# Stick-breaking attention in a two-layer streaming encoder: one query block at a time against two

## The chip, the cores and the metric

The kernel runs on one core of a Trainium2 chip. The metric is the device time of one launch in microseconds. The core has five engines with queues of their own: TensorE (PE, with its weight loads PEld), VectorE (DVE), ScalarE (ACT), GpSimd (POOL) and SyncE (SP, which here only issues transfers). TensorE writes to PSUM, which has eight banks of 512 fp32 columns each.

## The reference

Two layers run over 512 prompt tokens and 32 sample tokens together (544 columns in the kernel). In each layer one input projection feeds four token mixers (stick-breaking attention, retention, forgetting attention "fox", and sparse attention "dsa" on the 128 keys that an indexer selects), whose outputs are gated and summed; then come an output projection, a layer norm, a feed-forward and a second layer norm. The part that matters is the stick-breaking mixer, 4 heads of 64, with queries and keys in blocks of 128:

```
z = einsum('bqhd,blhd->bhql', q, k) * 64 ** -0.5
earlier = kpos[None, :] < qpos[:, None]
log_1mb = where(earlier, log_sigmoid(-z), 0.0)
after = cumsum(log_1mb, axis=3, reverse=True) - log_1mb      # sum over the later keys
w = where(earlier, exp(log_sigmoid(z) + after), 0.0)
y = einsum('bhql,blhd->bqhd', w, v)
```

Since `log_sigmoid(z) = z + log_sigmoid(-z)`, the exponent is `z` plus a sum of `log_sigmoid(-z)` over this key and all later ones, up to the query.

## The kernel before

**Precision.** Most products use the form fp32r, with each operand split in a high and a low part: a product is then two or three matmuls of the split parts. Each of these matmuls comes with its own load of 128x128 weights (the columns PE and PEld of the page have the same number of instructions).

**The stick-breaking mixer** (`stick`, line 1434). Keys stand on the partitions, queries on the free axis. For a query block `i` (128 queries), heads are taken in two passes `s` (0, 1), each with two heads `p`. The key blocks `j = i .. 0` are taken two at a time in "units"; a unit has one PSUM bank `z`, with 256 columns (2 heads x 128 queries) for each key block. In a unit:

- TensorE writes the mask (`sbmask`, bf16, only for the diagonal block) and, per key block and head, the logits: two matmuls of 128 columns (`sq` against the high part `sk` and the low part `skl` of the keys).
- `stick_unit` (line 1421) makes `log(1+exp(z))`: ACT Abs, Exp and Ln, a DVE operation (`sa`), an ACT copy to the high part of `hl` and a POOL subtraction for the low part of `hl`.
- `select` lets DVE do two steps of the indexer's top-k that waits to be done.
- TensorE adds the suffix sums to the same bank: the triangle `trin` against the block's own `hl`, and the all-minus-one matrix `onen` against the `hl` of every later key block, each for the high and the low part, 256 columns a time.
- ACT takes Exp to `sw`; the bank is then free for the next unit.

After both passes, `sw` and the values `svt` are multiplied in bank 7 (`so`), and `ev_heads` copies the result to `y_sb`. A unit's PSUM bank is one of two (`z=(4, 5)` in `BANKS`, line 106), which the indexer, fox, dsa and retention use too.

**The order of the work.** The program is recorded, not issued at once: every call becomes an entry with the entries it depends on, and `Plan.schedule` (line 553) sorts all of them for all engines by priority (the place in the program, less an offset), its own costs and the moment when operands are ready. So the stick mixer's matmuls stand between those of the projections that follow (fox, dsa). Places in SBUF are chosen from a draft of the same plan, so a change in one mixer can move entries anywhere. `Plan.fillers` (line 635) puts small bf16 matmuls (`idle`, line 657) where the plan has TensorE waiting. Nearly all instructions are issued from line 659, so the trace is read by tile names.

Names that come up below: `whi`, `wlo` (split weights of a projection, 272 columns a matmul, one half of the 544 tokens), `wop` (weights of the Strassen products in gates and feed-forward), `wb` (branch weights in `merge`), `T`, `T_plain` (differences of the halves of h for the Strassen products, made on POOL in `h_differences`, line 1699), `ikh`, `ikl`, `iq` (indexer), `fu`, `pT` (fox softmax), `oc`, `kd`, `S`, `rk` (retention, line 1541), `C,lf` (cumulative forget sums). The first layer is layer 0, the second layer 1.

Of the kernel before, what the change touches and what calls it, by code (L numbers as in the profile page):

```python
# [14 lines left out]
AF = mybir.ActivationFunctionType  # L15
# [649 lines left out]
class Build:  # L665
# [768 lines left out]
    def stick(self, q, qb, k, svt):  # L1434
        nc = self.nc
# [3 lines left out]
        for i in range(4):  # L1439
            blocks = list(range(i, -1, -1))  # L1440
            units = [tuple(blocks[a:a + 2]) for a in range(0, len(blocks), 2)]
            W = {}
            for s in range(2):
                r = slice(s * 64, s * 64 + 64)
                later = []
                for un in units:
                    n = 256 * len(un)
                    z = self.tps("sz")
                    first = True
                    if i in un:  # L1450
                        nc.tensor.matmul(z[:, :256], self.B["ident"],
# [3 lines left out]
                    for x, j in enumerate(un):  # L1455
                        for p in range(2):
                            c = (2 * x + p) * 128
                            self.z(z[:, c:c + 128], q, ks, 2 * p + s, slice(i * 128, (i + 1) * 128),
                                   slice(j * 128, (j + 1) * 128), first, True)
                            first = False  # L1460
                    hl = self.stick_unit(z, n)
                    self.select(SELECT[1])
                    own = [(hl, 256 * x) for x in range(len(un))]
                    for x, j in enumerate(un):
                        for src, a, lhs in [(*own[x], self.trin)] + [(*b, self.onen) for b in later + own[:x]]:
                            for part in range(2):
                                nc.tensor.matmul(z[:, 256 * x:256 * x + 256], lhs, src[:, part, a:a + 256], start=False,
                                                 stop=True, skip_group_check=True)
                    later = later + own
                    w = self.w512("sw")  # L1470
                    nc.scalar.activation(w[:, :n], z[:, :n], AF.Exp)
                    for x, j in enumerate(un):
                        W[s, j] = (w, 256 * x)
            o = self.aps("so")
            for p in range(2):
                for s in range(2):
                    h = 2 * p + s
                    for j in range(i + 1):
                        w, a = W[s, j]
# [608 lines left out]
```

## Time and profile before

| | |
|---|---|
| median of 3 runs | 1942.51 us (1942.05 to 1944.62) |
| the profiled execution | 1938.36 us, its span 1936.6 us |
| TensorE busy | 1871.6 us of the span (97%), 14658 matmuls |
| VectorE, ScalarE, GpSimd busy | 1607.1 (83%), 1053.3 (54%), 498.8 us (26%) |
| mean granted TensorE clock | 0.995 of 2.4 GHz |

Times in the trace are microseconds from the span's start. A matmul's row gives its whole passage; matmuls overlap, so what one costs TensorE is the distance from its start to the next one's start. A number in brackets with an arrow is how long the engine sat idle before a row, and who released it. The layers' stick mixers lie at 88 to 160 us and at 1050 to 1126 us.

### The profile page before, as it was taken

To read this page: it belongs to the slowest core of one execution; us is meant where nothing else is said; L and a number is where in the kernel's file an instruction comes from. 1 tells how busy PE (TensorE), PEld (TensorE's weight loads), DVE (VectorE), ACT (ScalarE), POOL (GpSimd) and SP (SyncE) were. 2 spreads that over 40 slices of the span, in tenths; PEclk is the share of its full clock that TensorE was granted. 3 is DMA by queue.
4 is the path that set the end of the run, shared out by engine and by line. 5 is a ranking of instruction groups with operands and counts; after the bars stand their busy time and mean duration, and the time that the engine had idled before them with its cause. 6 is when DMAs were issued, how large, how long until landed. Compare 5 with 4: busy or idle time off the path is not lost.

```text
span 1936.6 us, 39257 instructions
## 1 busy us (share of the span) xinstructions
PE 1871.6 (97%) x14658; PEld 1815.8 (94%) x14658; DVE 1607.1 (83%) x3566; ACT 1053.3 (54%) x2183; POOL 498.8 (26%) x500
## 2 busy tenths in 40 slices
PE   9999999999999999999999999999999999999997
PEld 8998898999999999999989989999999999999996
DVE  5988768887879989988789796687788799899875
ACT  4465533555637656556465563365556475565552
POOL 0343031143441111321413421312434301114101
PEclk9999999999999999999999999999999999999999
DMA  8222243667542587776413222346665237777741
GB/s 229 79 64 81 55 101 75 153 142 163 145 124 77 135 195 174 170 180 169 130 23 95 60 84 68 78 107 159 151 154 155 86 86 169 188 174 175 171 114 47
DMA packets 387423, 241.38 MB, mean 125 GB/s; under 512 B 27272, under 2 KB 363576, under 8 KB 386976
## 3 DMA queue, kind: packets, MB, share of 16 engines
q1 hardware_dynamic: 361888, 193.78, 36.2%
q0 software_dynamic: 25344, 45.10, 13.8%
q8 instruction: 115, 1.88, 0.4%
q14 instruction: 76, 0.62, 0.1%
HBM read 183.69 MB, written 7.82 MB: 99 GB/s over the span
## 4 chain that ended last, share of the span: by engine, by line
PE 71%; DVE 17%; DMA 5%; ACT 4%; issue 3%; POOL 1%; SPq 1%; POOLq 0%; ACTq 0%; DVEq 0%
PE bank L659 70%; DVE wop L659 3%; DMA ws<-wa 3%; DVE lnw L659 2%; DVE y L659 2%; DVE wsum L659 1%; DVE wlo L659 1%; DVE st L659 1%; DVE q L659 1%; DVE score L659 1%; DVE fu L659 1%; SPq L659 1%; DVE su L659 0%; DVE sv L659 0%; ACT wop L659 0%
## 5 line engine op out<-in xcount | busy, mean ns | idle before, releaser
L659 PE MATMUL bank<-T,wop 128*128 128x272 f32 x3456 | 460.6, 289 | 4.6 <-DVE su L659 3.1
L659 PEld LDWEIGHTS bank<-T,wop 128*128 128x128 f32 x3456 | 443.3, 188 | 7.1 <-DVE su L659 4.3
L659 PE MATMUL bank<-h0hi,wop 128*128 128x272 f32 x1152 | 244.9, 291 | 0.3 <-DVE acc L659 0.3
L659 PEld LDWEIGHTS bank<-h0hi,wop 128*128 128x128 f32 x1152 | 190.0, 188 | 3.6 <-DVE acc L659 0.5
L659 POOL DMA_DIRECT2D wt<-raw x88 | 76.6, 870 | 370.8 <-DVE wop L659 68.2
L659 POOL DMA_DIRECT2D ws<-wa x88 | 76.9, 874 | 352.7 <-DVE wop L659 114.8
L659 ACT ACTIVATE wop<-raw 128x512 fp32r<-128x512 f32 (+1 forms) x176 | 108.9, 620 | 107.1 <-PE bank L659 96.2
L659 PE MATMUL bank<-h0lo,wop 128*128 128x272 f32 x576 | 165.7, 288 | 0.0
L659 PE MATMUL bank<-q,wop 128*128 128x272 f32 x1176 | 153.0, 290 | 4.4 <-DVE su L659 2.6
L659 PEld LDWEIGHTS bank<-q,wop 128*128 128x128 f32 x1176 | 148.8, 189 | 7.5 <-DVE su L659 3.6
L659 DVE TENSOR_TENSOR wop<-raw,wop 128x512 fp32r<-128x512 f32 (+1 forms) x176 | 126.0, 718 | 31.1 <-ACT wop L659 30.5
L659 ACT ACTIVATE wop<-wsum 128x512 fp32r<-128x512 f32 (+1 forms) x176 | 109.1, 620 | 73.7 <-PE bank L659 46.5
L659 PE MATMUL bank<-h0hi,whi 128*128 128x272 f32 (+1 forms) x480 | 146.0, 304 | 2.3 <-ACT h0hi L659 2.3
L659 DVE TENSOR_TENSOR wlo<-raw,whi 128x1024 fp32r<-128x1024 f32 (+1 forms) x92 | 123.7, 1351 | 27.8 <-PE bank L659 12.7
L659 PE MATMUL bank<-h1hi,whi 128*128 128x272 f32 (+1 forms) x480 | 142.3, 296 | 1.1 <-DVE iq L659 1.1
L659 ACT ACTIVATE whi<-raw 128x1024 fp32r<-128x1024 f32 (+1 forms) x92 | 95.5, 1049 | 87.2 <-PE bank L659 46.6
L659 PE MATMUL bank<-h0hi,wlo 128*128 128x272 f32 (+1 forms) x480 | 139.3, 290 | 2.0 <-DVE wlo L659 2.0
L659 PE MATMUL bank<-h0lo,whi 128*128 128x272 f32 (+1 forms) x480 | 139.2, 290 | 2.0 <-DVE h0lo L659 2.0
L659 DVE TENSOR_TENSOR wop<-wsum,wop 128x512 fp32r<-128x512 f32 (+1 forms) x176 | 122.2, 694 | 22.8 <-ACT wop L659 22.0
L659 PE MATMUL bank<-h1lo,whi 128*128 128x272 f32 (+1 forms) x480 | 138.5, 289 | 0.5 <-DVE h1lo L659 0.5
L659 PE MATMUL bank<-h1hi,wlo 128*128 128x272 f32 (+1 forms) x480 | 138.6, 289 | 0.0
L659 PE MATMUL bank<-h1hi,wop 128*128 128x272 f32 x576 | 121.4, 289 | 0.0
(452 smaller groups left out, 5076.7 us busy)
## 6 DMA issues: line engine op xcount, KB each, us to landing
raw<-in_w_in_dram SPq DMA_DIRECT2D x46, 512.0 KB, 3.8
ws<-wa POOLq DMA_DIRECT2D x80, 256.0 KB, 4.4
wt<-raw POOLq DMA_DIRECT2D x80, 256.0 KB, 4.0
raw<-in_w_ffn_in_dram SPq DMA_DIRECT2D x76, 256.0 KB, 3.6
raw<-in_w_in_dram SPq DMA_DIRECT2D x68, 256.0 KB, 3.5
wa<-in_w_ffn_in_dram SPq DMA_DIRECT2D x38, 256.0 KB, 3.5
ws<-in_w_ffn_in_dram SPq DMA_DIRECT2D x38, 256.0 KB, 2.9
wt<-in_w_ffn_in_dram SPq DMA_DIRECT2D x38, 256.0 KB, 4.2
```

Of the source, the lines that this page charges most:

```text
L659: call(*a, **k)
```

## The change

Query blocks are taken in pairs: `i0` is 0 or 2, and a unit is now one key block `j` for both query blocks `i0` and `i0+1`, from `j = i0+1` down to 0. For `j = i0+1` only the later query block sees the keys (`lo = 1`, 128 queries for each of two heads, 256 columns); for all others the unit has 256 queries for each head, 512 columns. A logit matmul has 256 columns instead of 128 where both query blocks take part, and a suffix-sum matmul 512 instead of 256. Where the later key block has only the second query block, its `hl` is added to the second half of each head, a strided output of 2 runs of 128 columns. The mask for `j = i0` is written to the first 128 columns of each head, strided too. The values product and its eviction are done for both query blocks after the pair's four (or eight) units.

```diff
-        for i in range(4):
-            blocks = list(range(i, -1, -1))
-            units = [tuple(blocks[a:a + 2]) for a in range(0, len(blocks), 2)]
+        for i0 in (0, 2):
             W = {}
             for s in range(2):
                 later = []
-                for un in units:
-                    n = 256 * len(un)
+                for j in range(i0 + 1, -1, -1):
+                    lo = 1 if j > i0 else 0
+                    w = 256 - 128 * lo
+                    n = 2 * w
                     z = self.tps("sz")
+                    zv = z[:, :n].rearrange("k (p q) -> k p q", p=2)
                     first = True
-                    if i in un:
-                        nc.tensor.matmul(z[:, :256], self.B["ident"],
+                    if j >= i0:
+                        nc.tensor.matmul(zv[:, :, :128], self.B["ident"],
...
-                    for x, j in enumerate(un):
-                        for p in range(2):
-                            c = (2 * x + p) * 128
-                            self.z(z[:, c:c + 128], q, ks, 2 * p + s, slice(i * 128, (i + 1) * 128),
-                                   slice(j * 128, (j + 1) * 128), first, True)
-                            first = False
+                    for p in range(2):
+                        self.z(z[:, p * w:(p + 1) * w], q, ks, 2 * p + s, slice((i0 + lo) * 128, (i0 + 2) * 128),
+                               slice(j * 128, (j + 1) * 128), first, True)
+                        first = False
                     hl = self.stick_unit(z, n)
                     self.select(SELECT[1])
-                    own = [(hl, 256 * x) for x in range(len(un))]
-                    for x, j in enumerate(un):
-                        for src, a, lhs in [(*own[x], self.trin)] + [(*b, self.onen) for b in later + own[:x]]:
-                            for part in range(2):
-                                nc.tensor.matmul(z[:, 256 * x:256 * x + 256], lhs, src[:, part, a:a + 256], start=False,
-                                                 stop=True, skip_group_check=True)
-                    later = later + own
...
+                    for src, a, lhs in [(hl, lo, self.trin)] + [(*x, self.onen) for x in later]:
+                        sw = 256 - 128 * a
+                        for part in range(2):
+                            nc.tensor.matmul(zv[:, :, w - sw:], lhs,
+                                             src[:, part, :2 * sw].rearrange("k (p q) -> k p q", p=2), start=False,
+                                             stop=True, skip_group_check=True)
+                    later.append((hl, lo))
+                    e = self.w512("sw")
+                    nc.scalar.activation(e[:, :n], z[:, :n], AF.Exp)
+                    W[s, j] = (e, w, lo)
...
+            for i in (i0, i0 + 1):
+                o = self.aps("so")
...
+                            e, w, lo = W[s, j]
+                            a = p * w + (i - i0 - lo) * 128
+                            nc.tensor.matmul(o[:, h * 128:(h + 1) * 128], v[:, j, p * 128:(p + 1) * 128], e[:, a:a + 128],
+                                             start=j == 0, stop=j == i)
+                self.ev_heads(y, o, i * 128, 128)
```

Counted over the whole program (two layers): logit matmuls go from 160 of 128 columns to 32 of 128 and 64 of 256; suffix-sum matmuls from 160 of 256 columns to 16 and 32 (these strided) of 256 and 56 of 512; of the 16 mask matmuls 8 become strided. The values product, and every operation of DVE, POOL and the transfers, keep number and shape; ACT has 22 table loads instead of 24. Of the fillers the plan now has 220 instead of 241.

The order moves over the whole program. Three places, each as the engine's queue has it (an `x3` at the end is three such rows in a row; the number behind a name tells buffers apart).

TensorE, layer 0, the suffix sums of the last unit of the second pass (`hl_226` is that unit's own, `sqb` belongs to the sample tokens, `C,lf` to fox). Before:

```order
L659 MATMUL bank_64<-sqb_149,kccache_sb_k_229 128x64
L659 MATMUL bank_65<-hl_226,trin_75 128x256
L659 MATMUL bank_65<-hl_222,onen_77 128x256 x4
L659 MATMUL bank_65<-hl_226,trin_75 128x256 x2
L659 MATMUL bank_65<-hl_222,onen_77 128x256 x4
L659 MATMUL bank_65<-hl_226,onen_77 128x256 x2
```

In the change:

```order
L659 MATMUL bank_65<-hl_226,trin_75 128x512
L659 MATMUL bank_65<-hl_214,onen_77 128x2x128 x2
L659 MATMUL bank_65<-hl_218,onen_77 128x512 x2
L659 MATMUL bank_65<-hl_222,onen_77 128x512 x2
L659 MATMUL bank_64<-sqb_149,kccache_sb_k_229 128x64 x4
L659 MATMUL bank_66<-C_74,lf_120 4x512
```

The last unit took 13 matmuls of 256 columns here (a 14th, the first `trin`, stands earlier); now it has 7 (and an 8th earlier), six of them with 512 columns counting the earlier one, two with a strided output.

GpSimd, layer 0, the low parts `hl` of the units and the differences `T_plain` between them. Before:

```order
L659 TENSOR_TENSOR hl_190<-sa_188,hl_190 128x512
L659 TENSOR_TENSOR hl_194<-sa_192,hl_194 128x512
L659 TENSOR_TENSOR T_plain<-T_plain,h1lo_112 128x1088 x3
L659 TENSOR_TENSOR hl_198<-sa_196,hl_198 128x512
L659 TENSOR_TENSOR hl_202<-sa_200,hl_202 128x256
L659 MEMSET kccache_sb_k_229 128x2x96
L659 TENSOR_TENSOR hl_206<-sa_204,hl_206 128x512
```

In the change:

```order
L659 TENSOR_TENSOR T_plain<-h1hi_111 128x1088
L659 TENSOR_TENSOR hl_198<-sa_196,hl_198 128x256
L659 TENSOR_TENSOR T_plain<-T_plain,h1lo_112 128x1088
L659 TENSOR_TENSOR hl_202<-sa_200,hl_202 128x512
L659 TENSOR_TENSOR T_plain<-T_plain,h0hi_94 128x1088
L659 TENSOR_TENSOR T_plain<-T_plain,h1lo_112 128x1088
L659 TENSOR_TENSOR hl_206<-sa_204,hl_206 128x512
L659 TENSOR_TENSOR T_plain<-T_plain,h0lo_95 128x1088
L659 TENSOR_TENSOR hl_210<-sa_208,hl_210 128x512
```

The differences, which stood together behind two units' subtractions, now stand singly or in twos ahead of four of them.

TensorE, layer 1, the end of retention, where the first gate of `merge` is done and the second (`wop_1991`) is next. Before:

```order
L659 MATMUL bank_67<-S_1935,qd_1944 128x128
L659 MATMUL bank_67<-rvt_1907,A_1941 128x64
L659 MATMUL bank_66<-ident_70,oc_1940 128x128 x2
L659 MATMUL bank_67<-rvt_1907,A_1941 128x64
L659 MATMUL bank_61<-h0hi_1511,wop_1991 128x272
L659 MATMUL bank_61<-h0lo_1512,wop_1991 128x272
```

In the change (the lines left out are the rest of the 22 fillers in three places):

```order
L659 MATMUL bank_66<-ident_70,oc_1940 128x128 x2
L659 MATMUL bank_67<-rvts_1908,As_1951 32x64
L657 LDWEIGHTS idle_72
L657 MATMUL bank_60<-idle_72 128x128
...
L659 MATMUL bank_66<-ident_70,rk_2465_1883 128x128 x2
L659 MATMUL bank_66<-rvt_1907,kd_1942 128x128 x2
...
L659 MATMUL bank_66<-ident_70,oc_1948 128x128 x2
...
L659 MATMUL bank_61<-h0hi_1511,wop_1991 128x272
L659 MATMUL bank_61<-h0lo_1512,wop_1991 128x272
```

The second gate's matmuls now follow one chunk of retention later (`oc_1948` where it was `oc_1940`), and 22 fillers stand where gate matmuls stood. Before, layer 1 had no fillers there; layer 0 had, and has, such a place (26 before, 25 now).

## Rows read from the trace of the kernel before

**Rows 1.** The page: the span, each engine's busy time, share of the span and number of instructions, and the shares of the chain of work that ended last, by engine.

```profile
span 1936.6 us, 39257 instructions
PE 1871.6 (97%) x14658; PEld 1815.8 (94%) x14658; DVE 1607.1 (83%) x3566; ACT 1053.3 (54%) x2183; POOL 498.8 (26%) x500
PE 71%; DVE 17%; DMA 5%; ACT 4%; issue 3%; POOL 1%; SPq 1%; POOLq 0%; ACTq 0%; DVEq 0%
```

**Rows 2.** Busy time by stretches of 20 us; the columns are the stretch, its length, then PE, PEld, DVE, ACT and POOL busy with the number of instructions, the granted clock, the DMA share and GB/s. The first two lie in the stick mixer of layer 0, the third in the fox mixer behind it, the fourth in the stick mixer of layer 1.

```profile
100.00:120.00 20.00, 20.00 (x166) 19.99 (x165) 13.75 (x29) 14.53 (x32) 17.34 (x9) 1.00 0.23 62
120.00:140.00 20.00, 20.00 (x166) 19.68 (x165) 18.78 (x45) 12.12 (x24) 3.00 (x4) 1.00 0.20 55
180.00:200.00 20.00, 17.48 (x131) 15.37 (x131) 19.39 (x77) 11.14 (x33) 1.40 (x2) 1.00 0.37 91
1080.00:1100.00 20.00, 20.00 (x168) 19.90 (x167) 11.38 (x20) 9.43 (x20) 15.80 (x7) 1.00 0.20 54
```

**Rows 3.** The chain that ended last, in order of time (start, length, engine and what): its long pieces on TensorE around the stick mixers of layer 0 and layer 1, and where it next turns to TensorE.

```profile
58.79 30.63 PE bank L659 x238
...
98.74 56.40 PE bank L659 x444
...
162.02 20.98 PE bank L659 x174
...
1039.91 30.69 PE bank L659 x253
...
1075.78 42.17 PE bank L659 x332
...
1123.17 6.89 PE bank L659 x58
```

**Rows 4.** TensorE in order of time, logit matmuls of 128 columns of one unit: the first and the last of 15 in a row (start, duration).

```profile
143.91 0.28 PE L659 MATMUL bank<-sq,skl 128*128 128x128 f32 x1
...
145.47 0.27 PE L659 MATMUL bank<-sq,skl 128*128 128x128 f32 x1
```

**Rows 5.** TensorE in order of time, the indexer's matmuls of the same form with 256 and with 512 columns, each run up to the start of the next matmul.

```profile
42.79 0.28 PE L659 MATMUL bank<-ikl,iq 128*128 128x256 f32 x1
42.91 0.28 PE L659 MATMUL bank<-ikh,iq 128*128 128x256 f32 x1
43.02 0.28 PE L659 MATMUL bank<-ikl,iq 128*128 128x256 f32 x1
43.14 0.29 PE L659 MATMUL bank<-h0hi,whi 128*128 128x272 f32 x1
...
50.10 0.39 PE L659 MATMUL bank<-ikh,iq 128*128 128x512 f32 x1
50.34 0.39 PE L659 MATMUL bank<-ikl,iq 128*128 128x512 f32 x1
50.57 0.40 PE L659 MATMUL bank<-ikh,iq 128*128 128x512 f32 x1
50.80 0.39 PE L659 MATMUL bank<-ikl,iq 128*128 128x512 f32 x1
```

**Rows 6.** TensorE in order of time, two runs of suffix-sum matmuls of 256 columns (start, length of the whole run, number).

```profile
142.30 0.63 PE L659 MATMUL bank<-hl,onen 128*128 128x256 f32 x4
...
143.01 0.87 PE L659 MATMUL bank<-hl,onen 128*128 128x256 f32 x6
```

**Rows 7.** TensorE's groups by line and shape over the whole span (count, busy time, mean ns of one, idle time before them): values product, logits, suffix sums.

```profile
L659 PE MATMUL bank<-sw,svt 128*128 128x128 f32 x160 | 21.3, 280 | 0.0
L659 PE MATMUL bank<-sq,sk 128*128 128x128 f32 x80 | 19.6, 282 | 0.0
L659 PE MATMUL bank<-sq,skl 128*128 128x128 f32 x80 | 19.1, 276 | 0.0
L659 PE MATMUL bank<-hl,trin 128*128 128x256 f32 x80 | 18.3, 300 | 0.5 <-ACT hl L659 0.5
L659 PE MATMUL bank<-hl,onen 128*128 128x256 f32 x80 | 13.3, 280 | 0.0
```

**Rows 8.** Fillers: all of them by shape; and TensorE in order of time at the end of retention in layer 0, from the first filler to the matmul behind the last.

```profile
L657 PE MATMUL bank<-idle 128*128 128x128 bf16 x240 | 18.7, 235 | 2.8 <-DVE dq L659 1.5 <-DVE h0lo L659 0.8 <-ACT dq L659 0.6
...
313.62 0.44 PE L657 MATMUL bank<-idle 128*128 128x128 bf16 x5
315.32 0.44 PE L659 MATMUL bank<-ident,rk 128*128 128x128 f32 x2 [1.25 <-DVE y_ret L659]
315.60 0.89 PE L657 MATMUL bank<-idle 128*128 128x128 bf16 x13
316.38 0.71 PE L659 MATMUL bank<-rvt,kd 128*128 128x128 f32 x4
316.92 0.61 PE L657 MATMUL bank<-idle 128*128 128x128 bf16 x8
317.94 0.49 PE L659 MATMUL bank<-S,qd 128*128 128x128 f32 x2 [0.41 <-DVE S L659]
```

**Rows 9.** GpSimd in order of time in the stick mixer of layer 0 and one group of its operations over the span (ns min/median/max): differences and low parts.

```profile
107.70 7.62 POOL L659 TENSOR_TENSOR T_plain<-T_plain,h1lo 128x1088 f32<-128x1088 f32 x3
116.48 2.24 POOL L659 TENSOR_TENSOR hl<-sa,hl 128x512 fp32r<-128x512 f32 x2 [1.17 <-ACT hl L659]
...
L659 POOL TENSOR_TENSOR T_plain<-T_plain,h1lo x8: 2495/2540/3416, 60.6 to 1093.4; 128x1088 f32<-128x1088 f32 x8
```

**Rows 10.** A wait of TensorE in the indexer of layer 0: the row ahead of it and the row that waited.

```profile
56.05 0.29 PE L659 MATMUL bank<-h0hi,wlo 128*128 128x272 f32 x1
58.77 0.67 PE L659 MATMUL bank<-rls,C 128*32 128x288 f32 x2 [2.42 <-DVE score L659]
```

More of the change, by code (lines that the diff above doesn't have):

```diff
@@ L1438, in stick @@
         y = self.fm("y_sb")
-        for i in range(4):
-            blocks = list(range(i, -1, -1))
-            units = [tuple(blocks[a:a + 2]) for a in range(0, len(blocks), 2)]
+        for i0 in (0, 2):
             W = {}
             for s in range(2):
-                r = slice(s * 64, s * 64 + 64)
                 later = []
-                for un in units:
-                    n = 256 * len(un)
+                for j in range(i0 + 1, -1, -1):
+                    lo = 1 if j > i0 else 0
+                    w = 256 - 128 * lo
+                    n = 2 * w
                     z = self.tps("sz")
+                    zv = z[:, :n].rearrange("k (p q) -> k p q", p=2)
                     first = True
-                    if i in un:
-                        nc.tensor.matmul(z[:, :256], self.B["ident"],
+                    if j >= i0:
+                        nc.tensor.matmul(zv[:, :, :128], self.B["ident"],
                                          self.B["sbmask"][:, None, :].to_broadcast([128, 2, 128]), start=True,
@@ L1469, in stick @@
-                    later = later + own
[L1470 to L1479, printed above, removed]
-                        nc.tensor.matmul(o[:, h * 128:(h + 1) * 128], v[:, j, p * 128:(p + 1) * 128],
-                                         w[:, a + p * 128:a + (p + 1) * 128], start=j == 0, stop=j == i)
@@ L1482, in stick @@
-            self.ev_heads(y, o, i * 128, 128)
+                    for src, a, lhs in [(hl, lo, self.trin)] + [(*x, self.onen) for x in later]:
[4 more added lines that the diff above has]
+                                             stop=True, skip_group_check=True)
@@ new lines, in stick @@
+                    later.append((hl, lo))
[4 more added lines that the diff above has]
+                o = self.aps("so")
+                for p in range(2):
+                    for s in range(2):
+                        h = 2 * p + s
+                        for j in range(i + 1):
+                            e, w, lo = W[s, j]
[3 more added lines that the diff above has]
+                self.ev_heads(y, o, i * 128, 128)
```

## The prediction

> **What bounds the kernel now.** I read the page first: TensorE is busy for 97% of the span, and the chain that ended last lies on it for 71% [rows 1]. That share is a mean over stages, so the next view was the busy time in stretches of 20 us around the two stick mixers, the only place where the change edits work. There TensorE is busy for the whole 20.00 us and starts 166 or 168 matmuls in each stretch, which is one in 0.12 us [rows 2]. The chain by time says the same: between 58.79 and 162.02 us in layer 0 it lies on TensorE for 30.63 + 56.40 = 87.03 of 103.23 us, which is 84%; between 1039.91 and 1123.17 us in layer 1 for 30.69 + 42.17 = 72.86 of 83.26 us, which is 88% [rows 3]. So in these stages a matmul that is taken away should be worth its start-to-start time, less some 14% for stretches in which another engine ends last. Behind the stick mixer this no longer holds: in the fox mixer TensorE is busy 17.48 us of 20 with 131 matmuls, and DVE 19.39 [rows 2].
>
> **What the change takes away.** Only TensorE's work changes; DVE, POOL and the transfers do the same operations, and ACT, 54% busy, saves two table loads, for which I count nothing. The columns are the same too: logits 160 x 128 = 32 x 128 + 64 x 256 = 20480, suffix sums 160 x 256 = 48 x 256 + 56 x 512 = 40960. What falls is the number of matmuls, and the question is what one costs at each width.
>
> A logit matmul of 128 columns starts (145.47 - 143.91) / 14 = 0.111 us after the one before [rows 4]. The new logits of 256 columns are not in this trace, but the indexer's matmuls have their form (split operands, a weight load each): (43.14 - 42.79) / 3 = 0.117 us [rows 5]. So 128 columns cost nearly what 256 do. Before: 160 x 0.111 = 17.8 us. After: 32 x 0.111 + 64 x 0.117 = 11.0 us. Saved: 6.8 us.
>
> A suffix-sum matmul of 256 columns takes (0.87 - 0.63) / 2 = 0.12 us, from two runs of six and four [rows 6]; the nearest row with 512 columns is the indexer's, (50.80 - 50.10) / 3 = 0.233 us [rows 5]. Before: 160 x 0.12 = 19.2 us. After: 48 x 0.12 + 56 x 0.233 = 18.8 us. Saved: 0.4 us, since two of 256 cost as much as one of 512. The rows' counts agree with the code: 80 + 80 logits, 80 + 80 suffix sums [rows 7]. The values product keeps its 160.
>
> Together TensorE loses 7.2 us of work. With 86% of the two stretches on TensorE the gain is 7.2 x 0.86 = 6.2 us. Bounds: all of it, 7.2 us, if the other pieces of the chain move along too; nothing, if what follows absorbs it (a rival below).
>
> **The one operation that the trace does not show** is a matmul with a strided output: 32 suffix sums and 8 masks now write 2 runs of 128 columns. From below, it costs what the unstrided one does, 0.12 us. From above I take two matmuls of 128 columns, 2 x 0.111 = 0.223 us, so 40 x 0.10 = 4 us more. I take the lower end: the runs are 128 columns each, and the row nearest in columns is that of 256. The Trainium skill speaks against the change here: "PSUM — Partial Sum Buffer", section Specifications (TRN2), notes that any non-contiguous access pattern slows matmuls significantly. No row of before can test that; by it the gain would be about the rival's 2.7 us below instead of 6.2.
>
> **What the new order moves.** Every unit still needs z, three ACT operations, one on DVE, the two parts of `hl`, suffix sums, Exp, and there are twelve units and two banks as before, so the pipeline of banks is not shortened; I count zero for it. The values products now stand together at the end of a pair and share bank 7, so the second query block's wait for the first one's eviction; in layer 0 two `C,lf` matmuls stand between, and I count zero again.
>
> The fillers show where the plan lets TensorE wait. In layer 0 the end of retention has 26 of them, and from 313.62 to 317.94 us TensorE does nearly nothing else: 4.3 us, 0.166 us for each filler [rows 8]. In the change the same place in layer 1 gets 22, where gate matmuls stood: 22 x 0.166 = 3.7 us that TensorE may now lose there. Elsewhere 43 fillers go, so over the program there are 21 fewer, 3.5 us less of waiting at that price; at the least they are worth their own busy time, 18.7 / 240 = 0.078 us each, 1.6 us [rows 8]. A wait of 2.42 us in the indexer of layer 0, where TensorE stood still for DVE's scores [rows 10], may shrink, since the waiting matmul now stands after more projection matmuls. I let these gains and the loss cancel in the likeliest time and keep them for the range.
>
> **The sum.** For the profiled execution: 1938.36 - 6.2 = 1932.2 us, a span of 1930.4. That execution lies 4.15 us below the median of the runs, so for the median: 1942.51 - 6.2 = 1936.3 us. A measurement of this kernel tells about 0.2% from no change, 3.9 us: below 1938.6 is faster, above 1946.4 slower.
>
> **The rivals.**
>
> *The waits fall as well.* All of the above, and 21 fillers' worth of waiting less: 1936.3 - 3.5 = 1932.8 us. For it: fewer fillers. Against: fillers are only the plan's view, and POOL and DVE share work in ways it may not foresee.
>
> *Strided outputs are slow.* 4 x 0.86 = 3.5 us come back: 1942.51 - 2.7 = 1939.8 us, no measurable change. For it: nothing in this trace; against: the runs are long.
>
> *The saved time turns into waits further on.* The fox mixer behind the stick mixer is held by DVE, 19.39 of 20 us busy [rows 2], whose work does not shrink, and layer 1's retention has a new gap. If the gap's 3.7 us are not won elsewhere: 1940.0 us; if all is absorbed, 1942.5. For it: rows 2. Against: between 100 and 120 us DVE is busy only 13.75 us, so it can start earlier when TensorE delivers earlier.
>
> *Time goes by columns.* If a matmul of 256 columns took twice one of 128, the logits would cost 64 x 0.222 + 32 x 0.111 = 17.8 us as before, and only the suffix sums' 0.4 us would be saved: 1942.1 us. [...] The trace is against it: 0.111 and 0.117 us for 128 and 256 columns [rows 4, 5].
>
> *Slower: the suffix sums wait behind the differences on POOL.* A `T_plain` takes 2.54 us in the middle, and three of them held POOL from 107.70 to 115.3 us [rows 9]. Now one or two of them stand ahead of four subtractions that make a unit's low part. The second half of that unit's suffix sums waits for it, the unit's PSUM bank with it, and of the two banks the other may wait as well. Before, TensorE was covered: POOL is busy 17.34 and 15.80 us in the stretches 100 to 120 and 1080 to 1100, and TensorE 20.00 [rows 2]. If the cover, the fox projection's matmuls, is used up sooner, each uncovered difference costs 2.54 us. Four cost 10.2 us, from which the 6.2 us won turn into a measurable loss; with five, 1942.51 - 6.2 + 12.7 = 1949.0 us. Against it: 3 to 21 projection matmuls stand between the halves in layer 0 of the new order.
>
> That the change does not do what it says is not a rival: the counts of the new order are those of the code.
>
> **How the numbers follow.** The forecast gets 0.45, fewer waits 0.12, strided outputs 0.10, absorbed gain 0.15, columns 0.02, slower 0.16. Faster are the first two, 0.57; the next three are within 0.2%, 0.27; slower 0.16. The likeliest time is 1936.3 us, its own range 1932.8 to 1938.6. For 8 in 10 I go down to 1930, which is fewer waits with the 2.42 us of the indexer won too, and up to 1947, which holds the cases without change and the lower part of the slower one.
>
> **What would show it.** Right: 96 logit matmuls of which those of 256 columns start 0.117 us apart, suffix sums of 512 columns 0.233 us apart, strided ones 0.12, and some 3 us less between the start of the first stick unit and the chain's turn to fox in either layer, with the lead kept to the end of the layer. Wrong: strided rows 0.2 us apart; TensorE below 20.00 us in the stick stretches with `hl` on POOL as releaser (the slower rival); TensorE's idle time in layer 1's retention and in fox grown by what the stick mixer won (absorbed). The forecast falls if the rest of the program, which the plan reorders from the indexer on, gains or loses more than the 6 us at stake.

## The result, and the profile of the changed kernel

The changed kernel takes 1965.04 us (median of 3 runs, 1964.18 to 1970.96) against 1942.51 us: 22.5 us slower, a ratio of 1.0122 with a 95% interval of 1.0089 to 1.0154. The prediction said 1936.3 us, with a range of 1930 to 1947, so it is wrong in sign and its range does not hold the time. Of the runs reported below, one execution of the changed kernel with idle matmuls (3945 us) and one of the old kernel at `HIPRI` 210 (7516 us) took far longer than the rest; the ratios leave them out, the medians count them and would be 1958.29 and 1948.41 us without.

The execution profiled is that of 1970.96 us, 32.6 us above the profiled one of before in its span. The first rows of its page answer to [rows 1].

```profile
span 1969.2 us, 39027 instructions
## 1 busy us (share of the span) xinstructions
PE 1885.9 (96%) x14517; PEld 1817.7 (92%) x14517; DVE 1604.9 (81%) x3566; ACT 1055.8 (54%) x2181; POOL 505.6 (26%) x500
```

Two things are to be seen. TensorE starts 141 matmuls fewer than before and is nevertheless busy 14.3 us longer (1871.6 in [rows 1]): a matmul at half clock counts for nearly two. With 272 columns they start 0.125 us apart at 98 us of this trace, at full clock, and 0.226 us apart at 995 us, at a clock of 0.50. And it stands idle for 1969.2 - 1885.9 = 83.3 us, before for 65.0, so 18.3 us more. 14.3 + 18.3 is the whole 32.6. The mean granted clock points to the same: 0.987 of full speed against 0.995, which is 25.6 us of lost clock over the span against 9.7.

Of the 22.5 us between the medians, the clock is a smaller part than these two profiles say, since the one of before is of a favourable execution. In 61 executions of the same kernel, timed beside the runs below, the mean clock was 0.989 to 0.994, on average 0.991, which is 17.5 us lost; the three executions of the changed kernel had 0.987, 0.989 and 0.990. By the middle one, 21.6 us lost, the clock accounts for some 4 us and not for 16.

**Where the time is.** I cut both traces at the same events: first logit matmul and last eviction of the stick mixer (`y_sb`) in either layer, first and last split of the merged branches (`mhl`), last low part of LN1 (`h0lo`) in layer 0, the indexer's second key split (`ikh`) in layer 1. These are the stretches of before. The columns are length, busy time and number of instructions of TensorE's matmuls, its weight loads, DVE, ACT and POOL, then the granted clock, the DMA engines' share and GB/s.

```profile
0.00:89.80 89.80, 83.89 (x649) 78.39 (x650) 62.75 (x152) 41.73 (x87) 18.63 (x19) 1.00 0.59 153
89.80:169.90 80.10, 79.67 (x644) 75.81 (x641) 65.52 (x147) 54.32 (x108) 38.41 (x26) 1.00 0.30 85
169.90:499.40 329.50, 317.07 (x2457) 302.74 (x2457) 260.08 (x632) 161.14 (x353) 81.31 (x90) 0.99 0.48 112
499.40:602.80 103.40, 100.86 (x788) 99.01 (x788) 87.86 (x161) 58.67 (x113) 38.29 (x41) 1.00 0.44 120
602.80:998.70 395.90, 386.32 (x3063) 380.80 (x3061) 349.64 (x744) 230.95 (x476) 83.20 (x93) 1.00 0.61 148
998.70:1047.90 49.20, 44.76 (x333) 42.34 (x333) 45.80 (x108) 22.48 (x46) 15.35 (x8) 1.00 0.25 63
1047.90:1129.90 82.00, 81.28 (x663) 78.13 (x660) 67.23 (x146) 53.20 (x108) 40.00 (x27) 1.00 0.28 86
1129.90:1496.90 367.00, 359.32 (x2761) 345.49 (x2760) 299.09 (x698) 196.31 (x415) 99.11 (x107) 0.99 0.50 118
1496.90:1936.60 439.70, 418.40 (x3319) 413.13 (x3318) 369.08 (x788) 234.52 (x483) 84.53 (x92) 0.99 0.54 135
```

The same stretches of the changed kernel:

```profile
0.00:89.10 89.10, 84.53 (x650) 79.01 (x651) 63.53 (x153) 42.15 (x87) 17.64 (x19) 1.00 0.60 155
89.10:164.30 75.20, 74.73 (x573) 69.90 (x571) 60.84 (x134) 55.91 (x107) 41.41 (x28) 1.00 0.25 68
164.30:505.20 340.90, 326.38 (x2468) 309.03 (x2467) 266.83 (x644) 163.15 (x355) 77.65 (x88) 0.98 0.48 113
505.20:614.10 108.90, 103.98 (x789) 101.95 (x788) 90.24 (x162) 57.84 (x110) 38.72 (x42) 0.97 0.48 129
614.10:1017.50 403.40, 389.97 (x3058) 382.66 (x3056) 347.60 (x742) 230.71 (x479) 89.61 (x92) 0.99 0.58 142
1017.50:1065.00 47.50, 46.07 (x334) 43.73 (x333) 39.79 (x107) 22.44 (x46) 13.67 (x7) 0.96 0.26 65
1065.00:1137.80 72.80, 70.98 (x537) 65.80 (x535) 59.22 (x133) 53.53 (x105) 40.91 (x27) 1.00 0.24 68
1137.80:1525.00 387.20, 370.02 (x2840) 353.99 (x2838) 307.54 (x711) 194.18 (x413) 100.05 (x108) 0.99 0.49 117
1525.00:1969.20 444.20, 419.21 (x3283) 411.60 (x3283) 369.30 (x788) 235.93 (x484) 85.90 (x92) 0.99 0.54 134
```

Read line by line: the two stick mixers became shorter, by 4.9 and 9.2 us. Part of that is work that left the stretch: the edit removes 60 matmuls from each mixer, but 71 and 126 are gone, and 79 more stand in layer 1 between the mixer and the merge. At 0.12 us each, the 66 that only moved out of layer 1's mixer are some 8 of its 9.2 us. The other seven stretches together are longer by 46.7 us. In three places the number of matmuls says that the work is the same: merge to LN1 in layer 0, 788 and 789 matmuls, 5.5 us longer; from there to the indexer of layer 1, 3063 and 3058, 7.5 us longer; and the end, 3319 and 3283, 4.5 us longer. No matmul that the edit touches stands in any of them.

**Where TensorE stands still there.** TensorE in order of time at LN1 of layer 0 and at the start of layer 1 (in brackets the idle time before the row and what ended it), in the profile of the changed kernel:

```profile
588.19 1.25 PE L659 MATMUL bank<-lnw,ones 128*128 128x272 f32 x2 [3.14 <-ACT lnw L659]
...
991.04 2.18 PE L659 MATMUL bank<-lnw,ones 128*128 128x272 f32 x4 [3.23 <-POOL lnw L659]
```

The stretches of 20 us around the two, in the columns above:

```profile
580.00:600.00 20.00, 16.86 (x110) 16.21 (x109) 14.56 (x32) 6.20 (x12) 7.14 (x8) 0.83 0.17 40
...
980.00:1000.00 20.00, 16.39 (x99) 15.11 (x99) 12.93 (x34) 10.34 (x25) 7.28 (x2) 0.83 0.20 53
```

In both, TensorE waits some 3.2 us for the normalization's sums, the granted clock falls to 1.2 GHz toward the end of the wait (0.83 is the mean of 20 us), and 110 and 99 matmuls are started in 20 us; in before no stretch of 20 us between 540 and 1040 us has a clock below 1.00, and those of the same times hold 144 and 133 matmuls. The clock does not always fall behind such a wait: before has one of 3.01 us at 1021.03 (shown further down), in a stretch at full clock.

### The profile page after: what moved, and what is told of

The parts are those of the page before. It is cut to its first block, busy times and chain, and to the rows that moved or that the text cites. A ratio compares the mean times of both kernels' runs of the same rounds, so it can differ in the third digit from the quotient of the medians.

```text
span 1969.2 us, 39027 instructions
## 1 busy us (share of the span) xinstructions
PE 1885.9 (96%) x14517; PEld 1817.7 (92%) x14517; DVE 1604.9 (81%) x3566; ACT 1055.8 (54%) x2181; POOL 505.6 (26%) x500
## 3 DMA queue, kind: packets, MB, share of 16 engines
q0 software_dynamic: 25344, 45.10, 13.6%
## 4 chain that ended last, share of the span: by engine, by line
PE 31%; DVE 10%; DMA 3%; ACT 3%; issue 2%; POOL 1%; SPq 0%; POOLq 0%; ACTq 0%; DVEq 0%
PE bank L659 31%; DMA ws<-wa 2%; DVE wop L659 1%; DVE lnw L659 1%; DVE y L659 1%; DVE st L659 1%; DVE wsum L659 1%; DMA raw<-in_w_ffn_out_dram 0%; DVE fu L659 0%; DVE wlo L659 0%; DVE T L659 0%; DVE q L659 0%; DVE su L659 0%; DMA cs<-in_consts_dram 0%; DMA ws<-in_w_ffn_out_dram 0%
```

## The prices of the matmuls, as the changed kernel shows them

TensorE in order of time: logits of 256 columns and the row behind them; suffix sums with a strided output (`onen`, 256 columns, two runs of 128) and the row behind; one suffix sum of 512 columns and the row behind.

```profile
98.95 0.28 PE L659 MATMUL bank<-sq,skl 128*128 128x256 f32 x1
99.06 0.28 PE L659 MATMUL bank<-sq,sk 128*128 128x256 f32 x1
99.18 0.28 PE L659 MATMUL bank<-sq,skl 128*128 128x256 f32 x1
99.30 0.38 PE L659 MATMUL bank<-sw,svt 128*128 128x128 f32 x2
...
96.55 0.39 PE L659 MATMUL bank<-hl,onen 128*128 128x256 f32 x2
96.79 0.28 PE L659 MATMUL bank<-bsbmask,bident 128*128 128x256 bf16 x1
...
107.10 0.40 PE L659 MATMUL bank<-hl,trin 128*128 128x512 f32 x1
107.33 0.40 PE L659 MATMUL bank<-hl,onen 128*128 128x256 f32 x2
```

The logits start (99.30 - 98.95) / 3 = 0.117 us apart, as predicted. The strided suffix sums take (96.79 - 96.55) / 2 = 0.12 us, as the unstrided ones did, so the rule of the Trainium skill, "PSUM — Partial Sum Buffer", Specifications (TRN2), that a non-contiguous pattern slows matmuls significantly, does not hold for two runs of 128 columns. A suffix sum of 512 columns takes 0.23 us. TensorE's groups by shape (count, busy time, mean ns of one, idle time before them and what ended it) answer to [rows 7]:

```profile
L659 PE MATMUL bank<-sw,svt 128*128 128x128 f32 x160 | 20.8, 279 | 1.1 <-DVE y_sb L659 0.9 <-ACT sw L659 0.2
L659 PE MATMUL bank<-hl,trin 128*128 128x512 f32 x32 | 13.5, 420 | 0.9 <-POOL hl L659 0.8
L659 PE MATMUL bank<-sq,sk 128*128 128x256 f32 x32 | 9.2, 309 | 0.3 <-ACT sw L659 0.3
L659 PE MATMUL bank<-hl,onen 128*128 128x256 f32 x32 | 6.4, 280 | 0.0
```

The waits that the pairing puts into the mixers themselves are small: 0.8 us for POOL's low parts, 0.9 us of values products for the bank that the first query block's eviction frees.

## The experiments

**Another placement in SBUF.** The planner draws up four placements, one for each pair in `FITS`, and takes the one whose planned end is lowest. (A planned end is the sum of the planner's own costs, not a time of the chip; I use it only to compare orders.) It took (10, 2) for the old kernel and (5, 5) for the new. Four runs fix the pair. The edit, with another pair in each:

```diff
-FITS = ((10.0, 5.0), (5.0, 5.0), (10.0, 2.0), (10.0, 10.0))
+FITS = ((10.0, 2.0),)
```

> The changed kernel, with one thing altered: buffers in SBUF are placed by the third pair of the table FITS, (10, 2), which is the pair that the planner picked for the kernel before; for the changed kernel it had picked the second, (5, 5). The planned ends differ little: 1876.6 us with this pair, 1874.2 us with the other, 1873.9 us for the kernel before. Theory A (the loss comes from the order and the places that the planner happened to choose, and not from the stick edit): most of the 22.5 us go, so 1935 to 1952 us. Theory B (the stick edit itself costs the time, for instance by its longer-lived buffers or its waits): the placement does not matter, 1960 to 1970 us.

Measured: 1957.81 us, 1.0091 of before (1.0072 to 1.0111).

> The changed kernel with the first pair of FITS, (10, 5); planned end 1875.0 us. Theory A (order and places): a time that need not be that of the run with (10, 2), anywhere from 1932 to 1965 us, since the plan's own ends do not tell the pairs apart. Theory B (the edit): 1960 to 1970 us.

Measured: 1960.34 us, 1.0098 (1.0077 to 1.0119).

> The kernel before, without the change, with the second pair, (5, 5), which the changed kernel uses; planned end 1891.1 us instead of 1873.9. Theory A (order and places): slower than before by 10 us or more, 1950 to 1975 us. Theory B (the edit): the measured time follows the planned end or stays, 1940 to 1960 us; it would be no more than 17 us above before.

Measured: 1971.62 us, 1.0161 (1.0119 to 1.0203).

> The kernel before with the first pair, (10, 5); planned end 1875.2 us, only 1.3 us above that of before. Theory A (order and places): the time differs from before by more than the plan says, by 5 to 25 us in either direction. Theory B (the edit): within 4 us of before, 1940 to 1947 us.

Measured: 1944.62 us, 1.0020 (1.0003 to 1.0038).

Neither theory stands alone. The old kernel without the change can be slowed by 29.6 us through its placement, where the plan says 17 (its four executions scatter from 1962 to 1983 us); but three placements of the new one all lie at 1958 to 1965 us. At fixed pairs the new kernel is some 16 us slower than the old with (10, 5) and with (10, 2), and 6.6 us faster with (5, 5), where the intervals of the two overlap.

**Idle matmuls ahead of the measured waits.** The clock fell behind waits, so I filled them. In the issue loop, with a table `MORE` of places and counts from each kernel's own profile:

```diff
-            for call, a, k in self.ops[i].calls:
+            for c, (call, a, k) in enumerate(self.ops[i].calls):
+                for j in range(MORE.get((i, c), 0)):
+                    self.real.tensor.matmul(out, x, x, start=False, stop=True, skip_group_check=True)
                 call(*a, **k)
```

> The changed kernel in its own order, with 730 idle matmuls of 128 columns more: ahead of each of the 52 TensorE instructions that waited over 0.4 us in its profile, as many as take about 0.1 us less than that wait (0.06 us each). Order, places in SBUF and all other work stay. In the profile of the changed kernel TensorE runs at half clock in ten stretches, 41 us together, and falls 26.3 us behind the plan inside them; in that of before in two, 10.2 us, and 8.2 us. Theory C (most of the loss is the half clock that follows such waits): the stretches go and with them 15 to 22 us, so 1943 to 1952 us. Theory A (the waits themselves, which another order brought, are the loss; the clock only follows): at most 5 us are won, 1960 to 1966 us. If the idle matmuls stand in the way of work: slower than 1966 us.

Measured: 1960.53 us, 1.0096 (1.0077 to 1.0115).

> The changed kernel with SBUF placed by the pair (10, 2), which measured 1957.81 us, with 660 idle matmuls more, put ahead of the 40 waits of over 0.4 us of that kernel's own profile. Theory C (half clock): it loses 27.4 us inside half-clock stretches, against 8.2 us in before; without them 1957.8 less 15 to 24 us, 1934 to 1943 us. Theory A (waits): 1953 to 1959 us.

Measured: 1965.65 us, 1.0133 (1.0116 to 1.0150).

> The kernel before, unchanged, with 580 idle matmuls more ahead of its own 48 waits of over 0.4 us. Theory C (half clock): at most the 8.2 us that it loses inside its two half-clock stretches, so 1934 to 1940 us. Theory A (waits): 1940 to 1944 us. If it lands where the changed kernel with such matmuls does, the pairing itself is worth nothing at equal clock; if the changed one is 6 us below it, the saved TensorE work is real and the clock alone hid it.

Measured: 1954.75 us, 1.0071 (1.0054 to 1.0089).

Theory C fell in the form in which I had it: the new kernel won 4.5 us of the 15 to 22, which is within the intervals of the two runs, and the other two lost 7.8 and 13.6. The trace of the old kernel with idle matmuls shows why the test itself was poor. TensorE in order of time at the start of layer 1:

```profile
1024.84 5.30 PE L666 MATMUL bank<-idle 128*128 128x128 bf16 x48 [3.81 <-DVE sq L667]
1030.07 0.72 PE L667 MATMUL bank<-rls,C 128*32 128x288 f32 x2
```

and the same place in before:

```profile
1021.03 0.65 PE L659 MATMUL bank<-rls,C 128*32 128x288 f32 x2 [3.01 <-DVE rls L659]
```

The 48 idle matmuls were meant to run in a wait of 3.01 us. They waited themselves, 3.81 us for DVE, and then ran for 5.30 us at half clock in front of the matmul whose operand was ready. So these runs do not measure what the clock is worth.

**TensorE's work taken away, and nothing moved.** The plan stays; at issue the matmuls on the low parts of the prompt's suffix sums are left out.

```diff
+                            nc.skip.add(len(nc.ops) - 1)
...
-                call(*a, **k)
+                if i not in self.skip:
+                    call(*a, **k)
```

> The kernel before with its order, places and idle matmuls exactly as planned, but 80 matmuls left out when the order is issued: the half of the suffix sums of the prompt's stick units that takes the low parts (256 columns each, 0.12 us, so 9.6 us of TensorE's work; the result then lacks the low parts' contribution). It asks what TensorE's work in the stick mixers is worth when nothing else moves. By the prediction's factor of 0.86: 8.3 us faster, 1934 us. Absorbed (fox, held by DVE, and later stages wait for others anyway): 0 to 3 us faster, 1939 to 1943 us. Slower, if the idle time brings half clock: above 1944 us.

Measured: 1938.54 us, 0.9987 of before (0.9976 to 0.9998), 2.6 us faster. Its trace, cut at the first logit matmul and the last eviction of either mixer, in the columns of the tables above:

```profile
0.00:92.30 92.30, 86.83 (x651) 81.39 (x651) 62.90 (x152) 41.99 (x87) 18.59 (x19) 0.96 0.57 149
92.30:169.60 77.30, 75.20 (x604) 71.11 (x601) 65.77 (x147) 54.14 (x108) 39.52 (x26) 1.00 0.30 89
169.60:1048.00 878.40, 850.07 (x6636) 826.59 (x6634) 741.28 (x1640) 472.72 (x986) 219.75 (x231) 1.00 0.52 126
1048.00:1126.20 78.20, 77.03 (x623) 73.44 (x620) 66.80 (x146) 53.39 (x108) 40.02 (x27) 1.00 0.29 90
1126.20:1933.30 807.10, 779.07 (x6078) 758.84 (x6076) 668.81 (x1485) 431.52 (x897) 183.78 (x199) 0.99 0.52 127
```

The mixers take 77.3 and 78.2 us where before took 80.1 and 82.0, so 2.8 and 3.8 us of the 4.8 us removed from each: 69%. Between the medians of the whole program 2.6 of 9.6 us are left, 27%, where I had put 86%; the interval allows 0.4 to 4.7 us. That is the time of the absorbed rival, but these traces do not show its mechanism. The stretch between the mixers takes 878.4 us (before 329.5 + 103.4 + 395.9 + 49.2 = 878.0) and the one behind them 807.1 (before 367.0 + 439.7 = 806.7), so the 6.6 us are nearly kept. What this execution loses lies ahead of the first mixer, where no matmul was left out: 92.3 us instead of 89.8, at a clock of 0.96 instead of 1.00.

**Both kernels at other values of one constant.** `HIPRI` says how far ahead weight splits are drawn. Its value has nothing to do with the change, but it reorders the program. Here the planner chooses the placement again: for the old kernel (10, 2) at 220 and (10, 5) at the other values, for the new one always (5, 5). With (10, 5) at 220 the old kernel measured 1944.62 us (above), so its placement is not what sets 220 apart. With 200 for the first pair of runs, 180, 190 and 210 for the others:

```diff
-HIPRI = 220
+HIPRI = 200
```

> The kernel before with one constant of the planner altered: HIPRI, by which weight splits are drawn ahead in the order, 200 instead of 220. Planned end 1877.0 us (1873.9 with 220). So far the measured time lay above the planned end by 68.1 and 69.4 us for two placements of the kernel before, by 80.5 for the third, and by 81.2, 85.4 and 90.8 us for three placements of the changed kernel. Theory D (the excess over the plan is a lottery of the order, the same for both kernels): 1877.0 plus 68 to 91, so 1945 to 1968 us. Theory E (the paired mixer itself brings some 16 us of excess; the kernel before does not have it): 1877.0 plus 68 to 70, so 1945 to 1947 us.

> The changed kernel with HIPRI 200. Planned end 1866.2 us, 10.8 us below that of the kernel before with the same constant; with 220 the two plans end within 0.3 us of each other. Theory D (the pairing saves its 6 us and more in the plan, and 220 was a value at which the old program happens to be planned unusually well): the changed kernel is faster than the kernel before at the same constant by 5 to 15 us; its own time 1866.2 plus 68 to 91, 1934 to 1957 us. Theory E (the pairing brings excess of its own): 1866.2 plus 81 to 91, 1947 to 1957 us, not faster than the kernel before with 200.

> The kernel before with HIPRI 180. Planned end 1880.6 us. Theory D: 1949 to 1972 us. Theory E: 1880.6 plus 68 to 70, 1949 to 1951 us.

> The changed kernel with HIPRI 180. Planned end 1867.0 us, 13.6 us below that of the kernel before with 180. Theory D: 1935 to 1958 us and 5 to 18 us faster than the kernel before with 180. Theory E: 1867.0 plus 81 to 91, 1948 to 1958 us, within 4 us of the kernel before with 180 or slower.

> The kernel before with HIPRI 190; planned end 1876.4 us. With 200 and 180 it lay 76.6 and 81.5 us above its plan, with 220 only 68.1. If 220 is an unusually good value for the old program: 1876.4 plus 75 to 82, 1951 to 1958 us. If not: 1944 to 1947 us.

> The changed kernel with HIPRI 190; planned end 1866.7 us, 9.7 us below that of the kernel before with 190. With 200 and 180 it was faster than the kernel before at the same value by 3.9 and 6.0 us, with 220 slower by 22. If the pairing is worth some 5 us and the value 220 is the exception: 2 to 8 us below the kernel before with 190, and 1866.7 plus 83 to 89, 1949 to 1956 us. If 200 and 180 were luck: above the kernel before.

> The kernel before with HIPRI 210; planned end 1878.2 us. If 220 is an unusually good value for the old program: 1878.2 plus 75 to 82, 1953 to 1960 us. If the neighbourhood of 220 is good: 1946 to 1948 us.

> The changed kernel with HIPRI 210; planned end 1869.4 us, 8.7 us below that of the kernel before with 210. If the pairing is worth some 5 us and 220 is the exception: 1 to 8 us below the kernel before with 210, and 1869.4 plus 81 to 90, 1950 to 1959 us. If the pairing itself brings the loss: above the kernel before.

Measured, in us, with the ratio to the kernel before at 220 and its interval:

| HIPRI | planned end, old / new | old | new | new - old |
|---|---|---|---|---|
| 180 | 1880.6 / 1867.0 | 1962.10, 1.0111 (1.0094 to 1.0127) | 1956.06, 1.0072 (1.0049 to 1.0096) | -6.0 |
| 190 | 1876.4 / 1866.7 | 1952.99, 1.0067 (1.0044 to 1.0090) | 1954.54, 1.0072 (1.0046 to 1.0098) | +1.6 |
| 200 | 1877.0 / 1866.2 | 1953.62, 1.0069 (1.0052 to 1.0085) | 1949.69, 1.0047 (1.0030 to 1.0064) | -3.9 |
| 210 | 1878.2 / 1869.4 | 1948.53, 1.0037 (1.0024 to 1.0049) | 1957.13, 1.0083 (1.0059 to 1.0106) | +8.6 |
| 220 | 1873.9 / 1874.2 | 1942.51 | 1965.04, 1.0122 (1.0089 to 1.0154) | +22.5 |

At the four other values the difference is -6.0 to +8.6 us, and the means over them are 1954.3 us for the old kernel and 1954.4 for the new: no gain of the pairing shows. Four differences that scatter over 15 us do not exclude the 6 us of the forecast either; only at 210 are the intervals of the two kernels apart. The value 220 is the best of the five for the old program and the worst for the new, 11.8 us below its mean and 10.7 above; these two are the 22.5 us. TensorE's idle time in the traces says the same: in the old kernel 65.0 us at 220 and 66.3 to 77.9 at the others, in the new one 83.3 and 72.5 to 76.9.

What stays at all five is that the new kernel runs further behind its plan: 83 to 91 us, the old one 69 to 82. Where the two measured times are alike, this is the same finding told from the plan's side: of the 9 to 14 us that the new plan is shorter at 180 to 210, at most 6 are executed. Theories D and E each had half: D gave the neighbours' times, E the excess. At 190 and 210 the new kernel came out above the old, which I had set down as the sign against a gain of some 5 us; and the old kernel at 210 lies nearer to what I expected if the neighbourhood of 220 is good than if 220 is an exception.

Part of the excess can be named. The two waits shown above, at LN1 and at the start of layer 1, stand in the traces of the changed kernel at all five values, with 3.10 to 3.17 us and 3.23 to 3.24 us. At 200, where it measured below the old kernel, in order of time:

```profile
580.80 0.70 PE L659 MATMUL bank<-lnw,ones 128*128 128x272 f32 x2 [3.10 <-ACT lnw L659]
...
978.91 2.18 PE L659 MATMUL bank<-lnw,ones 128*128 128x272 f32 x4 [3.24 <-POOL lnw L659]
```

In the old kernel TensorE's longest wait for `lnw` is 1.0 us at 220 and at most 2.3 us at the other values. So the two belong to the changed kernel's orders, but as the other values have them too, they are not by themselves what makes 220 its worst value. The clock behind them differs: at 200 no stretch from 578 to 586 us is below full clock, where at 220 the granted clock fell.

**Idle matmuls by the plan's rule.**

```diff
-    WARM = 0.55, 3.41
+    WARM = 0.8, 3.41
```

> The changed kernel with the planner's own rule for idle matmuls asking for more: WARM = 0.8 instead of 0.55, so 535 idle matmuls instead of 219, all in gaps that the plan itself foresees; order and places stay. With idle matmuls put ahead of measured waits the changed kernel won 4.5 us and the kernel before lost 13. If half clock is what keeps the plan's gain from being executed: 1965 less 5 to 15 us, 1950 to 1960 us. If the waits are: 1961 to 1968 us. If idle matmuls only stand in the way: above 1968 us.

Measured: 1961.42 us, 1.0115 (1.0096 to 1.0135), 3.6 us below that with 0.55, which the intervals do not tell from no change.

> The kernel before with WARM = 0.8: 524 idle matmuls instead of 240, in gaps that the plan foresees. It has two half-clock stretches of 10.2 us together and loses 8.2 us inside them. If half clock decides: 1934 to 1939 us. If not: 1939 to 1946 us. If idle matmuls stand in the way, as the 580 ahead of measured waits did: 1946 to 1957 us.

Measured: 1947.45 us, 1.0039 (1.0020 to 1.0057), 7 us worse than with 0.55. More idle matmuls do not bring the plan's gain back. As in the runs above, some of them wait: TensorE's idle time just before idle matmuls is 8.6 us in the old kernel with 0.8, and 2.8 us in [rows 8].

Apart from the one that leaves out the low parts, no kernel tried was faster than the one before.

## Why the prediction was wrong, point by point

**What bounds the kernel.** That TensorE is busy throughout the stick stretches was read rightly, and the stretches did become shorter. Wrong was the step from there to the end: "a matmul that is taken away should be worth its start-to-start time, less some 14%". Where one thing was changed and nothing moved, the mixers gave back 69% of the work removed and the program 27%. The share of a chain that lies on an engine tells who is waited for now; it does not tell how far the next limit is. That fox, with DVE at 19.39 of 20 us [rows 2], takes up the gain, as the rival had it, is not shown: in that run's trace the stretches behind the mixers are each only 0.4 us longer than before.

**What the change takes away.** All prices held: 0.117 us for 256-column logits, 0.23 for 512-column suffix sums, 0.12 for the strided ones. The 7.2 us of TensorE's work are gone. The rivals of strided outputs and of columns fall with these rows, and the slower rival (suffix sums behind `T_plain`) with the 0.8 us that TensorE waited for `hl` on POOL.

**What the new order moves.** This is the step that failed: "I let these gains and the loss cancel". I priced the new order by its fillers, 21 fewer and so less waiting. TensorE's idle time grew by 18.3 us instead, and the seven stretches outside the mixers by 46.7 us, against 14.1 us that the mixers became shorter. The plan itself had no gain to offer: its ends are 1873.9 us before and 1874.2 with the change, although 7.2 us of TensorE's work are gone. Fewer fillers did not mean a shorter plan. The place that I named, the end of layer 1's retention, has its 22 fillers, in three groups:

```profile
1303.81 0.45 PE L657 MATMUL bank<-idle 128*128 128x128 bf16 x5
...
1305.98 1.00 PE L657 MATMUL bank<-idle 128*128 128x128 bf16 x15
...
1307.57 0.28 PE L657 MATMUL bank<-idle 128*128 128x128 bf16 x2
```

From the first filler to the matmul behind the last, at 1308.19, they take 4.4 us against the 3.7 I had put there: the size was nearly right, and the place is one among many. Others had no filler, as the plan has no wait there: 3.14 us at LN1, 3.23 us at the start of layer 1, in this trace each with half clock behind it. Fillers show the waits that the plan knows; time was also lost in those it does not know.

**The rivals and the range.** The absorbed rival came nearest: it ended at no change, and the mean difference over the other four values of `HIPRI` is no change. Its mechanism is not shown. The remaining 22 us had no rival. The text names them ("if the rest of the program, which the plan reorders from the indexer on, gains or loses more than the 6 us at stake") as something that would make the forecast fall, but gives them neither a price nor a chance. The price could have been bounded from a row: TensorE's 65 us of idle time in before are all the waits that an order had hidden badly, and an edit that redraws the order redraws them all.

**What stays open.** How the larger excess divides between the half clock and the waits ahead of it was not separated, since the idle matmuls waited too. Set against the plan's own start times, which no row here shows, the new kernel falls back 26.3 us inside its half-clock stretches and before 8.2, which would be most of the difference; but the profile of before is a favourable one (a clock of 0.995, where 61 other executions have 0.989 to 0.994), and the placement (10, 2) falls back 27.4 us and is 7 us faster. So I do not call it shown. Why 220 suits the old program and not the new was not found; that it does is shown by its four neighbours only, and the two waits for `lnw` alone are not the reason.

## What to carry to other kernels

Where a planner orders the program, an edit has two prices: that of its instructions, which rows tell to some per cent, and that of the order that it brings, which here made -6 to +22 us of an edit that takes 7 us from TensorE. Put the second one into the range, with the spread that the planner's other settings give, and compare old and new at several settings before calling an edit good or bad. Before counting on a gain, look whether the planner's own end moves: here it did not, and at the settings where it moved by 9 to 14 us at most 6 were executed. And do not take work removed from a full engine for time saved: where nothing else moved, 69% of it showed in its own stage and 27% (4 to 49%) at the end.

## What the runs showed of the hardware

**GpSimd waits through a run of VectorE's instructions.** GpSimd's `lnw` operations of LN1 and LN2 (ns min/median/max) over the span of before:

```profile
L659 POOL TENSOR_TENSOR lnw<-lnw,lnw x42: 759/850/2496, 565.2 to 1557.3; 128x272 f32<-128x272 f32 x42
```

The same in the changed kernel, and one of its rows in order of time, two operations of which the first is the long one:

```profile
L659 POOL TENSOR_TENSOR lnw<-lnw,lnw x42: 754/858/6524, 573.0 to 1588.2; 128x272 f32<-128x272 f32 x42
...
983.62 7.36 POOL L659 TENSOR_TENSOR lnw<-lnw,lnw 128x272 f32<-128x272 f32 x2 [5.94 <-ACT lnw L659]
```

VectorE in order of time in the changed kernel beside that last row, the first, one in the middle and the last:

```profile
983.04 0.78 DVE L659 TENSOR_TENSOR h0lo<-y,h0hi 128x272 fp32r<-128x272 f32 x2
...
987.62 1.22 DVE L659 TENSOR_TENSOR wlo<-raw,whi 128x1024 fp32r<-128x1024 f32 x1
988.75 0.78 DVE L659 TENSOR_TENSOR h0lo<-y,h0hi 128x272 fp32r<-128x272 f32 x2
```

One operation that takes 0.85 us took 6.52, from 983.6 to about 990.1 us, while VectorE ran instructions with two operands in SBUF without a gap, up to 989.5 us. TensorE's wait of 3.23 us up to 991.04 ends with the second of the two. The traces of the changed kernel at the four other values of `HIPRI` have the same operation, 6.52 to 6.53 us long. The Trainium skill, "SBUF — State Buffer", section Summary: rules for kernel authors, says that a VectorE instruction with two SBUF inputs and a GpSimd instruction that reads SBUF block each other: the second to issue is held until the first has finished. That would be one instruction of VectorE, at most 1.2 us here; in these traces GpSimd got no turn until about the end of the whole sequence. The planner's costs, which let the two take turns, do not have this, and it is one of the waits that no filler covers.
